# An attention softmax whose bias step delivers the negated maximum itself

## The chip, the cores and the metric

The kernel runs on one core of a Trainium2 chip. A core has a matrix engine (TensorE: PE in the profile, with its weight loads as PEld), a vector engine (VectorE, DVE), a scalar engine for activation functions (ScalarE, ACT), a general engine (GpSimd, POOL) and a sync engine (SP) that issues DMAs. Each engine works through a queue of its own in order; semaphores hold an instruction until what it reads is there or what it overwrites is free. The metric is the device time of one launch in microseconds (us), lower is better.

## The reference

One layer of a bidirectional encoder over 4096 tokens of width 1024. After a norm and one large input projection, two groups of heads work side by side: an mLSTM matrix memory in both directions, and windowed attention. Their outputs go through an output projection, a residual add and a last norm. The change touches the softmax of the windowed attention alone:

```
scores = einsum('bnqhgd,bnkhd->bnhgqk', qb, kw) * (B_HEAD_DIM ** -0.5)
scores = where(mask, scores + bias, NEG_INF)
m = maximum(max(scores, axis=-1), sink_l)
p = exp(scores - m[..., None])
denom = sum(p, axis=-1) + exp(sink_l - m)
out = einsum('bnhgqk,bnkhd->bnqhgd', p, vw) / denom
```

There are 32 blocks of 128 queries, 8 query heads that share 2 key heads, and each block sees its own and the two neighbouring blocks of keys. Each head has a learned logit, the sink, that takes part in the maximum and in the denominator.

## The kernel before

The kernel has three passes. Pass 1 (lines 168 to 678) normalises the input, projects q, k and v of the attention, and runs the attention. Pass 2 computes the memory's projections and its backward states, pass 3 the forward states, the gates and the output projection. The products use an fp32 value split into two parts (three matmuls for one product), which is why PE has so many.

The attention runs in 64 *slots*, one for each block of queries `n` and key head `kv` (`sl = 2n + kv`). `slot` (line 442) deals the pieces of three slots in turn, so that a slot's scores are computed two slots ahead of its transposes, and its products with the values one slot after them:

- `att_a(sl, g)`, four times in a slot: the scores of one group of 128 rows (two query heads by 64 queries). Two matmuls (line 379) fill one of two PSUM buffers `sp`; a DVE step (line 382) adds the table of position biases, writes the sums to an SBUF tile `s`, and gives each row's maximum through an accumulator that a second small instruction writes out. After the fourth group a DVE step (line 389) takes the minimum of the negated maxima and the negated sink, 128x4 values, into `NG`; then ACT (line 391) runs the exponential of the four groups one after another, with `NG` as its bias and the row sums as its accumulator.
- `att_t(sl, i)`, up to three times: four transposes on PE (line 411), then a rounded copy on ACT (413) and the remainder on DVE (414), both into a tile `pt`.
- `att_o(sl, i)`, up to three times: two matmuls with the values (line 425) into the one PSUM buffer `op`. After the last of them a copy on ACT (437) and an add on DVE (438) bring the result into `ab`, of which there is one buffer for both key heads; after the second key head SP issues its store to `at_d` in HBM (440).

These pieces are dealt between the projections of the next blocks of tokens (`interleave`, line 132): `qproj` (548), `kproj` (484), `vproj` (516, 517). Beside them the input of later blocks is prepared: ACT's squares (214), DVE (250) and POOL (251) give each row's scale; POOL stores it to HBM with one DMA for each 128 rows, a single value for each row (254, `rs_d`); SP loads it back spread over all partitions (261, `rsb`); POOL multiplies (266, `scale_raw`); ACT rounds (275) and POOL takes the remainder (276). Late in pass 1 DVE and ACT also prepare weights (683, 684) and gates (706 to 785); `sinks` (394) then adds the sink's share to the row sums, and DVE's reciprocal of them (785) opens pass 2.

The order of the work on PE is written out by hand. The order on all other engines, SP and POOL's DMAs included, comes from a planner that simulates the program when it is built: it takes what is ready by order in the program, with steps in a `high_priority` block put forward by `EV`, 400 places (lines 437 and 438 are in one). `behind(c, ins)` keeps instructions of the same engine behind a named one; `LAST["act"]` names the latest exponential, and the squares of line 214 and the weight casts of line 683 are kept behind it.

Of the kernel before, what the change touches and what calls it, by code (L numbers as in the profile page):

```python
# [9 lines left out]
F32 = mybir.dt.float32  # L10
F32R = mybir.dt.float32r
BF16 = mybir.dt.bfloat16
AF = mybir.ActivationFunctionType
ALU = mybir.AluOpType
# [14 lines left out]
def f32(ap):  # L29
    return ap.bitcast(F32)  # L30
# [54 lines left out]
def xtile(c, shape, dt, name):  # L85
    return c.xp.tile(shape, dt, tag="x4", name=name)
# [81 lines left out]
def pass1(c):  # L168
    nc, tc, A = c.nc, c.tc, c.A
    NB = 16  # L170
    with ExitStack() as es:
        wk = es.enter_context(tc.tile_pool(name="p1", bufs=1, reuse_waits="tile"))
        x_in, LAST = {}, {}
# [147 lines left out]
        def small_loads():  # L321
            r = {}
            r["gb"] = wk.tile([128, 2, 2, 4], F32, name="gb")
            nc.sync.dma_start(r["gb"], A["gate_b"].partition_broadcast(128).rearrange("p (a b d) -> p a b d", a=2, b=2))
            sink = r["sink"] = wk.tile([128, 2, 2, 2], F32, name="sink")
            for z in range(2):
                nc.sync.dma_start(sink[64 * z:64 * z + 64].rearrange("p a h m -> p (a h m)"),
                                  A["sink"][z].partition_broadcast(64))
            r["nsink"] = wk.tile([128, 2, 2, 2], F32, name="nsink")
            return [r[k] for k in ("gb", "sink", "nsink")]  # L330

        bias = []
# [25 lines left out]
        KK, Q, V, XT, ST = {}, {}, {}, {}, {}  # L358

        def att_a(sl, g):  # L360
            n, kv = sl // 2, sl % 2
            left, right = n > 0, n < NCH - 1
            jl, jr = (0 if left else 128), (384 if right else 256)
            b = (n + 1) // 2 if right else n // 2
            col = n * 128 - (b * 256 - 256)
            kk = KK[b]
            qb, qc = Q[n // 2], (n % 2) * 128
            half, m = g // 2, g % 2
            lo, hi = max(jl, 64 * half), min(jr, 320 + 64 * half)
            kept = lambda g: slice(max(jl, 64 * (g // 2)), min(jr, 320 + 64 * (g // 2)))  # L370
            if g == 0:
                st = wk.tile([128, 4], F32, tag="st", bufs=4, name=f"st{sl}")
                ST[sl] = ([], list(range(jl // 128, jr // 128)), st)
            ps, _, mx = ST[sl]
            ng, rs = c.NG[:, kv, n, :], c.R[:, n, kv, :]
            sp = c.ps("a", [128, 384], f"sp{sl}_{g}")
            qt = qb[kv * 2 + m][:, qc // 64 + half].rearrange("p z q -> p (z q)")
            for z in range(2):
                nc.tensor.matmul(sp[:, lo:hi], qt, kk[:, kv, z, col - 128 + lo:col - 128 + hi],  # L379
                                 start=(z == 0), stop=(z == 1))  # L380
            s = SB[half][(2 * sl + m) % 6]
            nc.vector.tensor_tensor_reduce(out=s[:, lo:hi], in0=sp[:, lo:hi],  # L382
                                           in1=bias[0][:, kv * 2 + m, lo - 64 * half:hi - 64 * half],
                                           op0=ALU.add, op1=ALU.max, scale=1.0, scalar=-3e38,
                                           accum_out=mx[:, g:g + 1])
            ps.append(s)
            if g < 3:
                return
            nc.vector.scalar_tensor_tensor(ng, mx, -1.0, nsink[:, kv].rearrange("p h m -> p (h m)"), ALU.mult, ALU.min)  # L389
            for g in range(4):  # L390
                LAST["act"] = nc.scalar.activation(ps[g][:, kept(g)], ps[g][:, kept(g)], AF.Exp, bias=ng[:, g:g + 1],  # L391
                                                   accum_out=rs[:, g:g + 1])

        def sinks():
            for kv in range(2):
# [6 lines left out]
        PT, AB, OP = {}, {}, {}  # L402

        def att_t(sl, i):
            ps, js, _ = ST[sl]
            if i >= len(js):
                return
            j = js[i]
            tp = c.ps("b", [128, 512], f"tp{sl}_{j}")
            for g in range(4):  # L410
                nc.tensor.transpose(tp[:, g * 128:(g + 1) * 128], ps[g][:, j * 128:(j + 1) * 128], c.ident)  # L411
            pt = PT[sl, i] = xtile(c, [128, 2, 512], F32R, f"pt{sl}_{j}")
            nc.scalar.copy(pt[:, 0, :], tp)  # L413
            nc.vector.tensor_sub(pt[:, 1, :], tp, f32(pt[:, 0, :]))  # L414
# [27 lines left out]
        def slot(sl):  # L442
            T = lambda i: (lambda: att_t(sl, i))
            O = lambda i: (lambda: att_o(sl - 1, i))
            Sc = lambda g: (lambda: att_a(sl + 2, g))
            p = [Sc(0), O(0), Sc(1), T(0), O(1), Sc(2), T(1), O(2), Sc(3), T(2)]
            if sl == 0:
                p = [Sc(0), Sc(1), T(0), Sc(2), T(1), Sc(3), T(2)]
            if sl + 2 >= 2 * NCH:
                p = [O(0), T(0), O(1), T(1), O(2), T(2)]  # L450
            return p
# [172 lines left out]
        gb, sink, nsink = small_loads()  # L624
# [15 lines left out]
        with behind(c, LAST["gather"]):  # L640
            load_rows(3)
        norm_rows(3, LAST["q"])
        interleave(kproj(1) + vproj(1) + transposes(2), [(lambda g=g, s=s: att_a(s, g)) for s in range(2) for g in range(4)])
        c.w2 = []
        with behind(c, LAST["gather"]):
# [1029 lines left out]
```

## Time and profile before

| | |
|---|---|
| median of 3 runs | 2187.8 us (2187.6 to 2189.53) |
| profiled execution, first to last instruction (span) | 2182.1 us |
| the median's time outside such a span | 5.7 us |
| instructions | 34919 |
| busy: PE, PEld | 2156.9 us (99%), 1872.4 us (86%) |
| busy: DVE, ACT, POOL | 1416.9 (65%), 1079.3 (49%), 567.7 us (26%) |
| mean granted TensorE clock | 0.998 |
| first and last sum step (line 382) | 35.6 and 572.0 us |

Of the profiled execution the span is what is known; what lies outside it is taken from the median of the runs. A row of the busy groups reads: line, engine, operation, tile written <- tiles read, shape, count | busy time and mean duration of one | idle time of the engine just before them, and what ended it. In a row of one line's instructions the three numbers behind the count are the shortest, median and longest duration in ns. A row of the timeline gives start, duration, engine, line and tiles, and in brackets the idle time before it with what released it.

### The profile page before, as it was taken

Reading aid. Unit: us, or ns where it says so; the run is one execution under the profiler, and the core shown is the slowest. Engines: PE = TensorE matmul, PEld = TensorE weight load, DVE = VectorE, ACT = ScalarE, POOL = GpSimd, SP = SyncE. Lnnn points to the kernel's source line nnn. Section 1 sums busy time; section 2 is a strip of 40 time slices with the busy share of each in tenths; the row PEclk is TensorE's granted clock in tenths of the full one; section 3 lists DMA queues with packets and bytes.
Section 4 is the critical chain, followed back from the end, with each engine's and each line's share of the span. In section 5 each row is a group of like instructions: output and inputs, shape, how many; then the busy total and the mean of one; then the engine's idle time right before and its main releaser. Section 6 shows DMA issues by size and latency. Waiting matters only on the chain. (4 is left out here: it accounts for less than half of the span.)

```text
span 2182.1 us, 34919 instructions
## 1 busy us (share of the span) xinstructions
PE 2156.9 (99%) x12226; PEld 1872.4 (86%) x12226; DVE 1416.9 (65%) x3041; ACT 1079.3 (49%) x2650; POOL 567.7 (26%) x918
## 2 busy tenths in 40 slices
PE   8999999999999999999999999999999999999998
PEld 7999999999898888888888888888888888888886
DVE  7678787788686566556567655555554443777786
ACT  7788788787554344334344544444443321333333
POOL 3555465550031121121112211121211111112222
PEclk9999999999999999999999999999999999999999
DMA  9655455332342454144357887677676998667775
GB/s 277 158 171 147 128 173 122 130 124 64 102 148 78 141 163 135 62 160 160 113 163 230 290 259 238 211 253 225 214 238 188 329 359 283 181 177 191 193 191 147
DMA packets 249132, 398.96 MB, mean 183 GB/s; under 512 B 21979, under 2 KB 128475, under 8 KB 248956
## 3 DMA queue, kind: packets, MB, share of 16 engines
q1 hardware_dynamic: 220544, 303.50, 45.4%
q0 software_dynamic: 28176, 92.96, 13.6%
q8 instruction: 96, 1.57, 0.3%
q14 instruction: 80, 0.66, 0.1%
q10 hardware_dynamic: 236, 0.27, 0.1%
HBM read 275.99 MB, written 120.67 MB: 182 GB/s over the span
## 5 line engine op out<-in xcount | busy, mean ns | idle before, releaser
L932 PE MATMUL up<-xb,w 128*128 128x512 f32 x1344 | 338.4, 396 | 0.0
L1443 PE MATMUL o<-wo,yo 128*128 128x512 f32 (+1 forms) x1356 | 312.8, 393 | 0.0
L1443 PEld LDWEIGHTS o<-wo,yo 128*128 128x128 f32 x1356 | 253.2, 188 | 59.7
L932 PEld LDWEIGHTS up<-xb,w 128*128 128x128 f32 x1344 | 243.8, 188 | 47.2
L950 DVE SCALAR_TENSOR_TENSOR qk<-U,cw,qk 128x512 f32<-128x512 f32 x256 | 189.2, 752 | 91.1 <-ACT qk L948 85.8
L548 PE MATMUL qp<-xT,wqb 128*128 128x256 f32 x1536 | 242.4, 288 | 0.1
L548 PEld LDWEIGHTS qp<-xT,wqb 128*128 128x128 f32 x1536 | 214.2, 190 | 8.7 <-DVE wqb L319 0.5
L1262 PE MATMUL op<-w,xs 128*128 128x512 f32 x720 | 202.3, 408 | 0.0
L1262 PE MATMUL zp<-w,xs 128*128 128x512 f32 x720 | 187.9, 401 | 0.7 <-DVE z L1272 0.7
L905 PE MATMUL v2p<-w,xb 128*128 128x512 f32 x672 | 157.6, 395 | 0.0
L1262 PEld LDWEIGHTS zp<-w,xs 128*128 128x128 f32 x720 | 130.9, 189 | 27.4 <-DVE z L1272 1.1
L414 DVE TENSOR_TENSOR pt<-tp,pt 128x512 fp32r<-128x512 f32 x188 | 129.1, 687 | 37.7 <-ACT pt L413 35.2
L905 PEld LDWEIGHTS v2p<-w,xb 128*128 128x128 f32 x672 | 126.1, 188 | 30.1 <-DMA xb<-xT_d 0.5
L391 ACT ACTIVATE s<-s,NG 128x320 f32<-128x320 f32 (+1 forms) x256 | 139.8, 548 | 11.4 <-DVE NG L389 10.8
L1262 PEld LDWEIGHTS op<-w,xs 128*128 128x128 f32 x720 | 126.7, 189 | 21.4
L413 ACT CAST pt<-tp 128x512 fp32r<-128x512 f32 x188 | 110.5, 588 | 69.9 <-PE tp L411 67.6
L382 DVE CUSTOM_DVE_ANT_0 s<-sp,G 128x320 f32<-128x320 f32 (+1 forms) x256 | 122.2, 478 | 32.6 <-PE sp L379 29.9
L1229 ACT ACTIVATE hs<-num,r 128x128 f32<-128x128 f32 x128 | 47.0, 368 | 174.3 <-DVE r L1226 153.6
L425 PE MATMUL op<-pt,v 128*128 128x512 f32 x376 | 120.6, 402 | 5.9 <-DVE ab L438 5.8
L379 PE MATMUL sp<-kk,q 128*128 128x320 f32 (+2 forms) x512 | 118.8, 313 | 0.7 <-DVE kk L501 0.6
L411 PE MATMUL tp<-ident,s 128*128 128x128 f32 x752 | 113.2, 273 | 0.3 <-DVE pt L414 0.2
L1252 POOL DMA_DIRECT2D y_d<-ya x32 | 19.4, 607 | 329.8 <-ACT ya L1251 181.8
(275 smaller groups left out, 4480.5 us busy)
## 6 DMA issues: line engine op xcount, KB each, us to landing
xc<-xT_d SPq DMA_DIRECT2D x64, 512.0 KB, 8.1
xs<-xT_d SPq DMA_DIRECT2D x120, 256.0 KB, 6.6
xT_d<-xT POOLq DMA_DIRECT2D x104, 256.0 KB, 5.0
xb<-xT_d SPq DMA_DIRECT2D x48, 514.0 KB, 8.0
E<-m_d SPq DMA_DIRECT2D x64, 256.0 KB, 4.9
W<-w_d SPq DMA_DIRECT2D x64, 256.0 KB, 5.9
y<-y_d SPq DMA_DIRECT2D x32, 512.0 KB, 3.4
out<-xr POOLq DMA_DIRECT2D x31, 512.0 KB, 3.7
```

What stands on the lines that cost most here:

```text
L379: nc.tensor.matmul(sp[:, lo:hi], qt, kk[:, kv, z, col - 128 + lo:col - 128 + hi], start=(z == 0), stop=(z == 1))
L382: nc.vector.tensor_tensor_reduce(out=s[:, lo:hi], in0=sp[:, lo:hi], in1=bias[0][:, kv * 2 + m, lo - 64 * half:hi - 64 * half], op0=ALU.add ...
L391: LAST["act"] = nc.scalar.activation(ps[g][:, kept(g)], ps[g][:, kept(g)], AF.Exp, bias=ng[:, g:g + 1], accum_out=rs[:, g:g + 1])
L411: nc.tensor.transpose(tp[:, g * 128:(g + 1) * 128], ps[g][:, j * 128:(j + 1) * 128], c.ident)
L414: nc.vector.tensor_sub(pt[:, 1, :], tp, f32(pt[:, 0, :]))
L425: nc.tensor.matmul(op, vt, pt[:, z, :], start=(i == 0 and z == 0), stop=(i == len(js) - 1 and z == 1))
L548: nc.tensor.matmul(qp, wq[k // 2][:, k % 2, w, m * 128:m * 128 + 128], x[k], start=(k == 0 and j == 0), stop=(k == KT - 1 and j == 2))
L905: nc.tensor.matmul(vp, a, wv[k // 2][:, k % 2, m, :], start=(k == 0 and j == 0), stop=(k == KT - 1 and j == 2))
L932: nc.tensor.matmul(up[:, 0:hi - lo], w[k // 2][:, k % 2, a, cs], x, start=(k == 0 and j == 0), stop=(k == KT - 1 and j == 2))
L950: nc.vector.scalar_tensor_tensor(acc, U[:, t:t + 512], cw[:, cm, t:t + 1], acc, ALU.mult, ALU.add)
L1262: nc.tensor.matmul(P[nm], XS[n](a, k), w[:, m, :], start=(k == 0 and j == 0), stop=(k == KT - 1 and j == 2))
L1443: nc.tensor.matmul(p, a[:, z, k, :], w[k // 2][:, k % 2, m, lo:hi], start=k == 0 and z == 1, stop=k == 3 and z == 0 and m == 0)
```

## The change

The sum step of line 382 now writes the negated sum (scale -1) and takes the minimum over it, starting from the negated sink of its rows, which it reads as one value for each partition; its accumulator is written to `NG` directly. The step of line 389 and the small tile `st` are gone. Each exponential follows its own sum step, with scale -1, instead of running after the fourth group.

```diff
             if g == 0:
-                st = wk.tile([128, 4], F32, tag="st", bufs=4, name=f"st{sl}")
-                ST[sl] = ([], list(range(jl // 128, jr // 128)), st)
-            ps, _, mx = ST[sl]
+                ST[sl] = ([], list(range(jl // 128, jr // 128)))
+            ps, _ = ST[sl]
...
             nc.vector.tensor_tensor_reduce(out=s[:, lo:hi], in0=sp[:, lo:hi],
                                            in1=bias[0][:, kv * 2 + m, lo - 64 * half:hi - 64 * half],
-                                           op0=ALU.add, op1=ALU.max, scale=1.0, scalar=-3e38,
-                                           accum_out=mx[:, g:g + 1])
+                                           op0=ALU.add, op1=ALU.min, scale=-1.0,
+                                           scalar=nsink[:, kv, half, m:m + 1], accum_out=ng[:, g:g + 1])
             ps.append(s)
-            if g < 3:
-                return
-            nc.vector.scalar_tensor_tensor(ng, mx, -1.0, nsink[:, kv].rearrange("p h m -> p (h m)"), ALU.mult, ALU.min)
-            for g in range(4):
-                LAST["act"] = nc.scalar.activation(ps[g][:, kept(g)], ps[g][:, kept(g)], AF.Exp, bias=ng[:, g:g + 1],
-                                                   accum_out=rs[:, g:g + 1])
+            LAST["act"] = nc.scalar.activation(s[:, kept(g)], s[:, kept(g)], AF.Exp, scale=-1.0, bias=ng[:, g:g + 1],
+                                               accum_out=rs[:, g:g + 1])
```

More of the change, by code (lines that the diff above doesn't have):

```diff
@@ L404, in att_t @@
         def att_t(sl, i):
-            ps, js, _ = ST[sl]
+            ps, js = ST[sl]
             if i >= len(js):
```

## The prediction

> **What bounds the kernel now.** I read the page first, then the busy time of each engine in long stretches, then who waited for whom on PE.
>
> ```profile
> span 2182.1 us, 34919 instructions
> ...
> PE 2156.9 (99%) x12226; PEld 1872.4 (86%) x12226; DVE 1416.9 (65%) x3041; ACT 1079.3 (49%) x2650; POOL 567.7 (26%) x918
> ```
> ```profile
> 35.00:120.00 85.00, 81.86 (x617) 78.57 (x616) 61.60 (x173) 66.59 (x180) 46.93 (x67) 0.98 0.75 189
> 120.00:480.00 360.00, 360.00 (x2744) 348.65 (x2742) 286.72 (x740) 288.58 (x761) 195.78 (x269) 1.00 0.45 135
> 480.00:600.00 120.00, 115.83 (x792) 105.54 (x791) 92.92 (x238) 81.65 (x210) 13.35 (x44) 1.00 0.29 94
> 600.00:2100.00 1500.00, 1497.88 (x7568) 1255.13 (x7567) 895.36 (x1750) 592.94 (x1403) 283.39 (x475) 1.00 0.64 199
> ...
> PE bps L336 <- POOL ohb L299: 6.4, 1, 6.4
> PE op L425 <- DVE ab L438: 5.8, 4, 2.5
> ```
>
> In the stretches the columns are busy PE, PEld, DVE, ACT and POOL, then the granted clock, the DMA share and GB/s. PE bounds the kernel: 99% of the span, and not one visible idle microsecond from 120 to 480, where most attention runs. DVE and ACT are at 80% there (286.72 and 288.58 of 360), so shortening them gains nothing by itself. What an edit to the attention steps can win is PE's idle time beside attention: 3.14 us in 35 to 120 and 4.17 us in 480 to 600. Of it 5.8 us are one wait: the matmul of line 425 needs its single PSUM buffer, which DVE's add of line 438 frees. The 6.4 us wait comes before attention. The span stands against a median of 2187.8 us; I add the 5.7 us outside the span to every result.
>
> **What the change removes.** 64 DVE instructions at line 389, and four exponentials stop waiting for the last of four sums.
>
> ```profile
> L382 DVE CUSTOM_DVE_ANT_0 s<-sp,G x256: 343/481/493, 35.6 to 572.0; 128x320 f32<-128x320 f32 x120, 128x192 f32<-128x192 f32 x4, 128x256 f32<-128x256 f32 x4
> ...
> L389 DVE SCALAR_TENSOR_TENSOR NG<-st,nsink x64: 144/162/1824, 39.6 to 572.9; 128x4 f32<-128x4 f32 x64
> ...
> L389 DVE SCALAR_TENSOR_TENSOR NG<-st,nsink 128x4 f32<-128x4 f32 x64 | 21.1, 330 | 1.5
> ...
> L391 ACT ACTIVATE s<-s,NG 128x320 f32<-128x320 f32 (+1 forms) x256 | 139.8, 548 | 11.4 <-DVE NG L389 10.8
> ```
>
> DVE loses 64 x 330 ns = 21.1 us, and ACT loses 10.8 us of waiting, both off PE's path: they lie beside a PE that is busy. The mean of 330 ns is twice the median of 162: some take 1.8 us, and one of those matters below. These 128x4 steps read two SBUF tensors, and the long ones lie under a POOL tensor step. [...]
>
> **What it adds.** The sum step of line 382 now reads its start value per partition. The trace has no such form; the nearest rows are steps with and without a per-partition scalar.
>
> ```profile
> L1022 DVE SCALAR_TENSOR_TENSOR C<-C,decay,kv x124: 331/343/351, 633.7 to 1167.4; 128x129 f32<-128x129 f32 x124
> ...
> L397 DVE TENSOR_TENSOR NG<-sink,NG 128x128 f32<-128x128 f32 x2 | 0.6, 289 | 1.2 <-ACT s L391 1.2
> ```
>
> 343 against 289 ns is about 55 ns. The other bound is 0: the old step also carries two constants. Below 0 I see no reason. I take 55, the row nearest in operands (PSUM, one SBUF tensor, one scalar): 256 x 0.055 = 14 us, so DVE's net is -7 us, or -21 us by the other bound. Row 1022 keeps within 20 ns over 124 steps, so a scalar from SBUF by itself makes no long steps. All this hides behind PE; where DVE is full for a slot, the four sums gain 0.22 us and the removed step gives back at least 0.15, so an uncovered slot costs under 0.1 us. The negated scale of sum and exponential, and the minimum for the maximum, change no count and no shape: 0. Exponentials and their accumulator reads stay 256 each.
>
> **What it moves.** The exponentials leave as four separate steps, not as a burst of some 2.2 us. They issue no DMA, but they stand in ACT's queue ahead of the copy of line 437, and after that copy come DVE's add (438) and the store on SP's queue (440). The steps queued behind the latest exponential by order of issue (the squares of line 214 and the weight casts of line 683) now name a nearer one; PE waits for neither in the table of waits: 0, and at most one exponential, 0.55 us, if that cover were gone. The largest visible PE wait is where this counts:
>
> ```profile
> 63.16 4.74 POOL L266 TENSOR_TENSOR xraw<-xraw,rsb 128x1024 f32<-128x1024 f32 x2 [15.68 <-DMA rsb<-rs_d]
> ...
> 63.82 1.74 DVE L389 SCALAR_TENSOR_TENSOR NG<-st,nsink 128x4 f32<-128x4 f32 x1
> ...
> 65.65 0.56 ACT L391 ACTIVATE s<-s,NG 128x320 f32<-128x320 f32 x1 [1.42 <-DVE NG L389]
> ...
> 65.94 0.62 PE L425 MATMUL op<-pt,v 128*128 128x512 f32 x2
> ...
> 68.87 1.14 POOL L254 DMA_DIRECT2D rs_d<-rstd  x2 [0.29 <-POOL rstd L251]
> 69.10 0.58 ACT L437 COPY ab<-op 64x512 f32<-64x512 f32 x1
> ...
> 69.72 0.69 DVE L438 TENSOR_TENSOR ab<-op,ab 64x512 f32<-64x512 f32 x1
> ...
> 70.44 0.33 SPq L440 DMA_DIRECT2D at_d<-ab  x1
> ...
> 79.91 0.58 ACT L437 COPY ab<-op 64x512 f32<-64x512 f32 x1 [2.70 <-DMA at_d<-ab]
> ...
> 80.53 0.68 DVE L438 TENSOR_TENSOR ab<-op,ab 64x512 f32<-64x512 f32 x1 [2.56 <-ACT ab L437]
> ...
> 81.27 0.98 PE L425 MATMUL op<-pt,v 128*128 128x512 f32 x2 [2.47 <-DVE ab L438]
> ...
> DMA to landing us min/median/max: 2.0/3.3/9.4
> ...
> 80.00:90.00 10.00, 8.73 (x53) 8.40 (x54) 5.75 (x17) 6.45 (x18) 6.65 (x9) 0.83 0.78 293
> ```
>
> Read it from the end. PE idles 2.47 us because the next copy into `ab` waits until the store of 70.44 has landed: 9.4 us after its issue, where the median store takes 3.3. POOL had issued two stores of single 4-byte values (`rs_d`) 1.6 us before it. The store was that late because the copy of 69.10 was late, though its matmuls ended at 65.94 + 0.62 = 66.56: ACT first stood 1.42 us for line 389, itself held for 1.74 us beside POOL, and then ran the burst. Without line 389, three of the four exponentials have gone before. ACT reaches the copy up to 1.42 + 3 x 0.55 = 3.07 us earlier, but not before 66.56; the store then leaves at 66.6 + 0.58 + 0.69 + 0.1 = 68.0, ahead of 68.87. Bounds: 68.0 and 70.44 (the planner may fill the place with other casts). With only the 1.42 us won it leaves at 69.0, just behind POOL's. I take the early side: the 1.42 us and one of the three exponentials suffice (1.97 against the 1.57 us between 68.87 and 70.44). At the median landing the buffer is free by 71.3, long before 77.2 (79.91 less 2.70), and the idle 2.47 us go.
>
> With them goes a clock drop: 0.83 over 10 us is 3.4 us at half speed, 1.7 us of work. [...]
>
> The second place is the end of the stage:
>
> ```profile
> 575.43 0.29 DVE L397 TENSOR_TENSOR NG<-sink,NG 128x128 f32<-128x128 f32 x1 [1.18 <-ACT s L391]
> ...
> 577.98 0.58 ACT L437 COPY ab<-op 64x512 f32<-64x512 f32 x1 [0.35 <-PE op L425]
> 578.31 1.74 DVE L785 RECIPROCAL R<-R 128x256 f32<-128x256 f32 x1
> 580.08 0.69 DVE L438 TENSOR_TENSOR ab<-op,ab 64x512 f32<-64x512 f32 x1
> ...
> 580.83 0.73 PE L425 MATMUL op<-pt,v 128*128 128x512 f32 x2 [2.19 <-DVE ab L438]
> ```
>
> DVE's add waits behind the 1.74 us reciprocal, whose chain starts at line 397 after the last burst. With the burst gone that chain starts at least 1.18 us sooner; if the reciprocal is then queued before the late work, the add starts at 578.56, 1.5 us earlier. If the order stays, 0. I take 1.0. The remaining waits (the 1 us near 550, where DVE is full of gate and weight work) I leave as they are: bounds -1.0 and +0.3.
>
> **Sum.** 2182.1 - 2.5 - 1.7 - 1.0 = 2176.9; plus 5.7 is 2182.6 us.
>
> **Rivals.** (B) The store stays behind POOL's: the planner puts casts of `xT` and `pt` where the burst was. For it: two such casts stand between burst and copy now, and all of ACT is dealt out by a planner I cannot see. Only the end gains: 2186.8 us.
>
> (C) Slower: an exponential queued ahead of the copy of line 437 holds it, since it now waits for its own sum, whose scores PE computes after the matmuls being copied.
>
> ```profile
> 247.81 0.67 PE L425 MATMUL op<-pt,v 128*128 128x512 f32 x2
> ...
> 248.51 0.51 PE L379 MATMUL sp<-kk,q 128*128 128x320 f32 x2
> ...
> 249.24 0.58 ACT L437 COPY ab<-op 64x512 f32<-64x512 f32 x1
> ...
> 249.48 0.48 DVE L382 CUSTOM_DVE_ANT_0 s<-sp,G 128x320 f32<-128x320 f32 x1
> ...
> 249.88 0.68 DVE L438 TENSOR_TENSOR ab<-op,ab 64x512 f32<-64x512 f32 x1
> ...
> 251.00 0.63 PE L425 MATMUL op<-pt,v 128*128 128x512 f32 x2
> ```
>
> The add ends at 250.56 and the next matmul starts at 251.00: 0.44 us of slack. An exponential behind the sum of 249.48 would run from 250.05 to 250.6, and the copy would be 1.36 us late: 0.9 us of PE idle in that slot. It decides once the copy is over 0.44 us late. In all 64 slots that is 59 us; in one of eight, 7.4 us: 2195.2. Against it: the copy and the add are issued with raised priority, and none of the slots from 120 to 480 stalls today, whatever lies beside them.
>
> (D) The busy PE hides waits: rows of matmuls overlap, so a wait under 0.2 us does not show. [...] If each of 64 slots hid 0.1 us that the spread exponentials free, 6.4 us more than the end's gain: 2180.4. Against it, two windows of steady work:
>
> ```profile
> 120.00:180.00 60.00, 60.00 (x459) 58.12 (x458) 47.47 (x122) 47.80 (x125) 31.29 (x40) 1.00 0.40 125
> ...
> 300.00:360.00 60.00, 60.00 (x458) 58.04 (x458) 49.74 (x127) 47.82 (x127) 35.66 (x49) 1.00 0.55 156
> ```
>
> The count of matmuls does not move while DVE and DMA do.
>
> **Chances.** The forecast 0.47, B 0.25, C 0.20, D 0.08. A measurement of this kernel cannot tell less than about 0.2% (4.4 us) from no change: below 2183.4 is faster. The forecast lies 0.8 us past that line; its own range is 2180.8 to 2184.7 (the end at 0 to 2.19, the first place between 2.5 and 4.2). I give it 0.33 faster, 0.13 the same, 0.01 slower; B 0.24 the same, 0.01 slower; C slower; D faster. Faster 0.41, same 0.37, slower 0.22. The range 2179.5 to 2191.0 takes in B, D and the mild half of C.
>
> **What would show it.** The clock over 80 to 90 us back at 1.00 and no PE idle there: the first place is right. `at_d` issued before `rs_d` but still landing in 9 us: the reading of POOL's stores is wrong. The reciprocal before 578.3: the second place. Sum steps of 540 ns: the scalar's price; spread up to 1.8 us: it contends with POOL. PE idle before line 425 between 120 and 480: C, and the forecast is wrong. New PE idle after 600, which no step here touches, would be the planner's reordering, and would make it wrong too.

## The result and the profile after

The changed kernel takes 2192.5 us (median of 10 runs, 2189.46 to 2197.11) against 2186.8 us of the kernel before on the same chip: 1.0028 times the time, with a 95% interval of 1.0017 to 1.0039. It is slower by 0.28%, where the forecast was 2182.6 us, with a gain as the likeliest of three outcomes (0.41). Its profiled execution took 2190.26 us, 1.7 us more than its span; its span is 6.5 us longer than before's. Its ten times form two groups of five, 2189.5 to 2190.6 us at a mean granted clock of 0.999 and 2194.4 to 2197.1 us at 0.997 or 0.998, and the profile is of the lower group.

The page after, and its busy time in the stretches that the prediction used (PE, PEld, DVE, ACT, POOL, granted clock, DMA share, GB/s):

```profile
span 2188.6 us, 34920 instructions
...
PE 2160.2 (99%) x12226; PEld 1872.1 (86%) x12226; DVE 1429.0 (65%) x2977; ACT 1089.2 (50%) x2650; POOL 566.3 (26%) x918
```
```profile
120.00:480.00 360.00, 358.70 (x2701) 344.43 (x2700) 290.32 (x686) 291.80 (x755) 191.52 (x265) 1.00 0.43 132
480.00:600.00 120.00, 114.66 (x776) 104.19 (x776) 93.63 (x229) 83.02 (x206) 15.23 (x45) 1.00 0.29 89
```

PE is still at 99%, and from 120 to 480 us it shows only 1.3 us of idle time, yet in those 360 us it runs 43 matmuls fewer than before (2701 against 2744). The time went where the idle column cannot show it. DVE has 64 instructions fewer and 12.1 us more to do. Two groups, in the view by line (busy time, mean) and then with their shortest, median and longest duration, say why:

```profile
L381 DVE CUSTOM_DVE_ANT_0 s<-sp,G,nsink 128x320 f32<-128x320 f32 (+1 forms) x256 | 138.1, 540 | 34.1 <-PE sp L378 29.3
...
L522 DVE TENSOR_TENSOR v<-vg,v 128x128 fp32r<-128x128 f32 x32 | 43.0, 1345 | 0.3 <-ACT v L521 0.2
```
```profile
L381 DVE CUSTOM_DVE_ANT_0 s<-sp,G,nsink x256: 407/550/555, 35.6 to 578.0; 128x320 f32<-128x320 f32 x120, 128x192 f32<-128x192 f32 x4, 128x256 f32<-128x256 f32 x4
...
L522 DVE TENSOR_TENSOR v<-vg,v x32: 281/1056/2469, 23.7 to 530.2; 128x128 fp32r<-128x128 f32 x32
```

The sum step went from 478 to 540 ns in the mean, close to its price. The other row is a step that the change never touched: the remainder of v (what is left of v after its rounded cast), which took 402 ns in the median before (28.4 us in all).

```profile
L527 DVE TENSOR_TENSOR v<-vg,v x32: 274/402/1911, 23.7 to 525.4; 128x128 fp32r<-128x128 f32 x32
```

PE issues the same 12226 matmuls in the same order in both kernels, so each can be compared by its start. The table gives, for matmuls of the products with the values and for the last matmul of all, how much later (+) or earlier (-) than in the kernel before they start, in us, in the profiled execution of each kernel named; the heads are the times of these matmuls in the kernel before. The fourth column is the slope between 132 and 435 us: by how much the lag grows in one block of four slots (33.6 us). The kernels e2 to e18 are those of the experiments below; in e4 PE has 66 matmuls between 49.6 and 76.6 us in another order, so there the products with the values are paired by their own order.

| kernel | at 54 | at 98 | slope per block | at 435 | at 587 | last |
|---|---|---|---|---|---|---|
| changed | +1.6 | -3.1 | +0.51 | +2.0 | +4.5 | +6.5 |
| e2 constant start | +2.0 | +0.9 | +0.46 | +5.5 | +7.8 | +8.2 |
| e4 rows later (softmax of before) | -0.2 | -3.3 | +0.02 | -3.1 | -1.2 | -1.3 |
| e5 held | +0.4 | -4.2 | +1.97 | +15.9 | +19.9 | +20.5 |
| e6 step kept | +0.5 | +1.3 | +0.48 | +5.6 | +7.8 | +8.3 |
| e7 v after add | +1.8 | +1.1 | +0.15 | +2.7 | +5.4 | +6.1 |
| e8 v on POOL | +1.5 | -3.2 | +0.16 | -1.6 | -0.1 | +1.0 |
| e9 fourth named | +1.7 | -3.0 | +0.51 | +2.1 | +2.1 | +2.9 |
| e14 all but rows | +0.5 | -3.2 | +0.16 | -1.7 | -2.3 | -1.8 |
| e15 step kept, constant | +0.1 | -0.9 | 0.00 | -0.9 | -0.9 | -1.0 |
| e17 e14 with constant | +0.3 | -2.9 | +0.04 | -1.6 | -1.7 | -0.9 |
| e18 e14 without held start | +1.8 | -3.1 | +0.15 | -1.6 | -2.3 | -1.0 |

The changed kernel thus loses 1.6 us before 54 us (at 45.3 us PE idles 1.59 us for `kk`, the split keys), wins 4.7 by 98 us, loses 5.1 in the ten blocks to 435 us, 2.5 more to the end of the attention, and 1.9 in the passes behind it. The gain is the first place of the prediction; here are its rows after, and the same ten microseconds as there:

```profile
67.55 0.62 PE L420 MATMUL op<-pt,v 128*128 128x512 f32 x2
...
69.52 0.58 ACT L432 COPY ab<-op 64x512 f32<-64x512 f32 x1
...
70.92 0.33 SPq L435 DMA_DIRECT2D at_d<-ab  x1
71.24 1.14 POOL L254 DMA_DIRECT2D rs_d<-rstd  x2
```
```profile
80.00:90.00 10.00, 10.00 (x77) 9.65 (x77) 7.86 (x19) 6.96 (x18) 6.57 (x14) 1.00 0.92 234
```

The store `at_d` now goes ahead of POOL's stores and lands 2.03 us after its issue instead of 9.4; the idle 2.47 us and the half clock (in the kernel before 0.50 from 82 to 85 us, and 1.00 again from 85) are gone. But it goes ahead by 0.32 us, not by the 0.9 that the prediction had, and later than before (70.92 against 70.44). The loss is seen best in one slot:

```profile
246.96 0.67 PE L420 MATMUL op<-pt,v 128*128 128x512 f32 x2
...
247.16 0.30 DVE L518 TENSOR_TENSOR vg<-vp,vg 128x144 f32<-128x144 f32 x1
247.26 0.56 ACT L386 ACTIVATE s<-s,NG 128x320 f32<-128x320 f32 x1
...
247.81 0.61 ACT L275 CAST xT<-xraw 128x512 fp32r<-128x512 f32 x1
...
248.32 0.30 ACT L521 CAST v<-vg 128x128 fp32r<-128x128 f32 x1
248.50 1.10 POOL L276 TENSOR_TENSOR xT<-xraw,xT 128x512 fp32r<-128x512 f32 x1
248.64 0.58 ACT L432 COPY ab<-op 64x512 f32<-64x512 f32 x1
...
248.69 1.05 DVE L522 TENSOR_TENSOR v<-vg,v 128x128 fp32r<-128x128 f32 x1
...
249.66 0.67 DVE L433 TENSOR_TENSOR ab<-op,ab 64x512 f32<-64x512 f32 x1
...
250.39 0.74 PE L420 MATMUL op<-pt,v 128*128 128x512 f32 x2
```

The same slot before, beside the rows that the prediction showed for it:

```profile
248.67 0.30 DVE L523 TENSOR_TENSOR vg<-vp,vg 128x144 f32<-128x144 f32 x1
...
249.66 1.08 POOL L276 TENSOR_TENSOR xT<-xraw,xT 128x512 fp32r<-128x512 f32 x1
249.72 0.30 ACT L526 CAST v<-vg 128x128 fp32r<-128x128 f32 x1
...
250.49 0.40 DVE L527 TENSOR_TENSOR v<-vg,v 128x128 fp32r<-128x128 f32 x1
```

Before, v's split (cast and remainder) stood behind the copy into `ab` and behind the add. After, it stands ahead of both. The remainder starts at 248.69 beside POOL's step of 248.50 and ends 0.14 us after that step (249.74 against 249.60); before it did the same (250.89 against 250.74), but started late in POOL's step, and the add was already ahead of it. Now the add of 249.66 is behind it, and the next matmul into `op` starts as soon as that add is done. The row of that matmul has no bracket: none of this wait shows as idle time of PE. The slot stands for all: from 120 to 480 us there are two remainders of v in each block, and one of the two comes directly behind an add in all ten blocks of the kernel before, and directly ahead of one in all ten of the changed kernel.

### The profile page after: what moved, and what is told of

It reads as the page before. It is cut to its first block, busy times and chain, and to the rows that moved or that the text cites. A ratio compares the mean times of both kernels' runs of the same rounds, so it can differ in the third digit from the quotient of the medians.

```text
span 2188.6 us, 34920 instructions
## 1 busy us (share of the span) xinstructions
PE 2160.2 (99%) x12226; PEld 1872.1 (86%) x12226; DVE 1429.0 (65%) x2977; ACT 1089.2 (50%) x2650; POOL 566.3 (26%) x918
## 5 line engine op out<-in xcount | busy, mean ns | idle before, releaser
L381 DVE CUSTOM_DVE_ANT_0 s<-sp,G,nsink 128x320 f32<-128x320 f32 (+1 forms) x256 | 138.1, 540 | 34.1 <-PE sp L378 29.3
L378 PE MATMUL sp<-kk,q 128*128 128x320 f32 (+2 forms) x512 | 118.5, 312 | 0.6 <-DVE kk L496 0.6
```

## The experiments

The first theory, Q: an exponential now stands ahead of the copy into `ab` (the prediction's rival C, at a small size). Theory P: the dearer sum makes DVE late. A third, M, came out of the first runs: with the burst gone, other work (v's split, casts) has come to stand ahead of the copy and the add.

### Exponentials put back in the text, and the sum without its pointer

e1 issues the four exponentials behind the fourth group in the program; e3 issues them in pairs; e2 leaves them as they are, and takes the pointer away, so that the sink is left out of the maximum (the pointer is the start value that the sum reads for each partition).

```diff
 e1
-            LAST["act"] = nc.scalar.activation(s[:, kept(g)], s[:, kept(g)], AF.Exp, ...)
+            for i in range(4) if g == 3 else ():
+                LAST["act"] = nc.scalar.activation(ps[i][:, kept(i)], ps[i][:, kept(i)], AF.Exp, ...)
 e3
+            for i in (g - 1, g) if g % 2 else ():
 e2
-                                           scalar=nsink[:, kv, half, m:m + 1], accum_out=ng[:, g:g + 1])
+                                           scalar=3e38, accum_out=ng[:, g:g + 1])
```

> The new sum step stays, but the four exponentials go again as one burst after the fourth sum. Theory Q (place in ACT's queue: an exponential wedged ahead of the copy into ab delays DVE's add and the next op matmul by some 0.1 to 0.25 us a slot): the steady loss of 0.5 us per block of four slots from 120 to 480 us is gone, the 1.6 us lost before 54 us is gone, and the time is 2184 to 2187, at or below the kernel before. Theory P (price: the sum step of 540 instead of 480 ns makes DVE late in each slot): the steady loss stays at about 0.5 us per block and the time is 2190 to 2193. Theory O (the planner merely orders things otherwise, with no link to either): anything from 2184 to 2194, with the difference in one or two places rather than steady.

> The changed kernel with a constant start value (3e38) for the minimum in place of the per-partition negated sink: the sink is left out of the row's maximum. The sum step should go back to about 481 ns and DVE lose some 15 us of busy time. Theory Q: the exponentials still stand ahead of the copies, the steady loss of 0.5 us per block stays, and the time is 2190 to 2193. Theory P: the steady loss goes and the time is 2183 to 2186. If both share it: in between, 2187 to 2189.

> The changed kernel with the exponentials issued two by two, after the second and the fourth sum. The third group's scores come right after the op matmuls, so in this version no exponential of the third group is issued ahead of the copy into ab. Theory Q: most of the steady loss goes (under 0.2 us per block), the gains at 80 us (4 us) and at 578 us (1.5 us) stay, and the time is 2182 to 2187. Theory P: loss of 0.5 us per block stays, 2190 to 2193.

Measured against the kernel before (2185.3): e1 2189.7 us, ratio 1.0019 (1.0010 to 1.0028); e2 2191.3, 1.0027 (1.0018 to 1.0037); e3 2190.5, 1.0024 (1.0014 to 1.0035). The slope stays at 0.45, 0.46 and 0.47 us per block. Taken at its word this is against Q and P both. But e1 and e3 did not do what they were to do, as the timeline of e1 shows:

```profile
242.66 0.55 DVE L381 CUSTOM_DVE_ANT_0 s<-sp,G,nsink 128x320 f32<-128x320 f32 x1
...
243.26 0.56 ACT L387 ACTIVATE s<-s,NG 128x320 f32<-128x320 f32 x1 [0.30 <-DVE NG L381]
```

Each exponential still starts right behind its own sum: the planner takes what is ready, and only the data (before, all four minima in one step) had made them a burst. So e1 and e3 leave the move untried. e2 did get its sum of 480 ns, and the slope is 0.46. But the rest did not stay as it was: the planner there also puts one exponential and one cast of `pt` ahead of the copy into `ab` in each block, where the changed kernel has them behind it. So the pointer's share of the 0.51 cannot be read from e2 alone.

### The move undone by force, the step kept, and v's split

```diff
 e5
+            if g < 3:
+                return
+            last = None
+            for i in (3, 0, 1, 2):
+                with behind(c, last):
+                    LAST["act"] = nc.scalar.activation(ps[i][:, kept(i)], ...)
+                last = last or LAST["act"]
 e6
-                                           scalar=nsink[:, kv, half, m:m + 1], accum_out=ng[:, g:g + 1])
+                                           scalar=nsink[:, kv, half, m:m + 1], accum_out=mx[:, g:g + 1])
+            nc.vector.scalar_tensor_tensor(ng, mx, 1.0, nsink[:, kv].rearrange("p h m -> p (h m)"), ALU.mult, ALU.min)
 e7 (called in att_o, right after the add)
+                def split():
+                    with behind(c, LAST.get("abc")), behind(c, LAST.get("abv")):
+                        nc.scalar.copy(vt[:, :, 0:64], vv)
+                        nc.vector.tensor_sub(vt[:, :, 64:128], vv, f32(vt[:, :, 0:64]))
 e8
-                nc.vector.tensor_sub(vt[:, :, 64:128], vv, f32(vt[:, :, 0:64]))
+                nc.gpsimd.tensor_tensor(out=vt[:, :, 64:128], in0=vv, in1=f32(vt[:, :, 0:64]), op=ALU.subtract)
```

> In e1 and e3 the traces show each exponential still starting right behind its own sum: the place in the program text does not hold it back, so neither of them undid the move. Here the exponential of the fourth group goes first and the other three are queued behind it, so all four leave as a burst after the fourth sum, while the separate step between sums and exponentials stays removed and the sum keeps its new form. Theory M (the move: with the burst gone, ACT does v's split and the casts ahead of the copy into ab, and DVE's residual of v, held beside POOL, ahead of the add): the steady loss of 0.5 us per block and the 1.6 us before 54 us go, the time is within 2 us of the kernel before (2184 to 2187). Theory P (the removed step or the dearer sum): the loss stays, 2190 or more.

> The new sum step (negated, minimum, started from the negated sink; about 540 ns) writes to the small tile as before, and the separate 128x4 step between sums and exponentials is kept, so the exponentials are a burst again by their data. Everything of the change but the removal and the move. Theory M: no steady loss; time within 1.5 us of the kernel before, and the 9.4 us landing at 80 us is there again. Theory P (price of the sum): the loss of 0.5 us per block is there, 2189 to 2192.

> The changed kernel, with only this edit: in the blocks of the main loop, v's split (ACT's cast of 0.3 us and DVE's residual of 0.95 to 1.05 us) is queued behind the next copy into ab and add, where the kernel before had it. Theory M with this very step as the cause: the add starts 0.3 to 1.0 us sooner in one slot of four, the steady loss falls from 0.5 to 0.1 to 0.2 us per block, the time is 2186 to 2188 (some 4 us below the changed kernel). If the cause is spread over all the casts: a quarter of that at most, 2190 to 2191.

> The changed kernel with DVE's residual of v (128x128, two SBUF inputs) moved to POOL, nothing else. It tests the price of the residual itself: in the changed kernel each of them ends 0.15 us behind the POOL step that runs beside it (median 1.05 us, was 0.40). Theory M: DVE's busy time falls by about 29 us, the add no longer stands behind it, the steady loss falls to 0.2 us or less per block, time 2186 to 2188; POOL's next steps are later by 0.3 to 1 us, which nothing waits for. If the held residual is not the cause: 2190 to 2192.

e7 measured 2187.5 us, ratio 1.0013 (1.0004 to 1.0022), and e8 2187.4, 1.0008 (0.9999 to 1.0017). In both the slope falls from 0.51 to 0.15 and 0.16 us per block, as theory M has it: one step, standing in front of the add, is 70% of the steady loss. e8 is the cleanest of all the runs: ACT's work is in the changed kernel's order in all 2650 places, v's cast still ahead of the copy, and DVE's is too but for the remainders that are gone. So it is the remainder on DVE that holds the slot, not the cast on ACT. The slot of above in e7, where the add no longer waits for it and the remainder itself takes 0.27 us:

```profile
251.84 0.68 DVE L433 TENSOR_TENSOR ab<-op,ab 64x512 f32<-64x512 f32 x1 [0.29 <-ACT ab L432]
...
252.44 0.27 DVE L527 TENSOR_TENSOR v<-vg,v 128x128 fp32r<-128x128 f32 x1
```

e7 also shows how narrow the gain at 80 us is. In its profiled execution `at_d` goes 0.56 us behind the first of POOL's stores and lands after 9.9 us, and the wait and the drop of the clock that the kernel before had there are back (ACT's copy waits 2.72 us for the store, and the clock is at 0.83 in the mean from 80 to 90 us, as before):

```profile
70.53 1.14 POOL L254 DMA_DIRECT2D rs_d<-rstd  x2
71.09 0.33 SPq L437 DMA_DIRECT2D at_d<-ab  x1
...
81.07 0.58 ACT L432 COPY ab<-op 64x512 f32<-64x512 f32 x1 [2.72 <-DMA at_d<-ab]
```
```profile
80.00:90.00 10.00, 7.58 (x44) 7.23 (x45) 4.87 (x14) 5.57 (x16) 5.59 (x12) 0.83 0.97 297
```

e5 fell out against every theory: 2203.8 us, 1.0086 (1.0072 to 1.0100). The slope is 1.97 us per block, and PE waits 15.3 us for `pt`:

```profile
PE tp L412 <- DVE pt L415: 15.3, 14, 1.2
```

The forced burst runs the last group first, which the kernel before did not, and DVE no longer has the order of before either; what of the 1.97 us is the burst and what the order was not separated. It does win 4.2 us by 98 us and lose only 0.4 before 54 us, which points to the exponentials as what costs the 1.6 us at the start; e11 and e14 below, which hold the exponentials of the first two slots alone, bear it out (0.0 and +0.5 us at 54 us).

By theory M e6 was to be as fast as the kernel before, and was not: 2193.0 us, 1.0032 (1.0020 to 1.0045). Its first three blocks from 132 us on take exactly as long as before (+1.3 us at 132 and at 235 us), then it loses 1.3 to 1.4 us each in three single blocks. Theory P, dismissed after e2, was back: with the step kept, DVE has to do both 540 ns sums and the step. e15, below, takes it up.

### The gain at 80 us alone

```diff
 e4 (kernel before)
+            rows = [lambda: norm_rows(b + 4, LAST["act"])]
-            A1 = slot(4 * b) + [lambda: norm_rows(b + 4, LAST["act"])]
+            A1 = slot(4 * b) + (rows if b else [])
-            A2 = slot(4 * b + 2) + slot(4 * b + 3)
+            A2 = slot(4 * b + 2) + ([] if b else rows) + slot(4 * b + 3)
```

> The kernel before, softmax untouched; only the first block's norm rows (whose rs_d stores of single 4-byte values stand ahead of the first at_d store) are issued one slot later than the first at_d. My reading of the place at 80 us: at_d lands in 2 to 4 us instead of 9.4, the 2.47 us of idle PE and the drop to half clock at 80 us go, and the time is 4 us below the kernel before (2182 to 2183). If the reading is wrong: at_d still lands in about 9 us, PE still idles at 78 to 81 us, and the time is the kernel before's within 1 us.

Measured 2181.7 us against 2185.3, ratio 0.9982 (0.9973 to 0.9991): about the forecast's own time, with the softmax untouched. `at_d` is issued ahead of `rs_d` by 11.6 us and lands after 2.08 us, and no idle time or half clock is left from 80 to 90 us:

```profile
68.88 0.33 SPq L440 DMA_DIRECT2D at_d<-ab  x1
...
80.51 1.11 POOL L254 DMA_DIRECT2D rs_d<-rstd  x2
```
```profile
80.00:90.00 10.00, 10.00 (x79) 9.69 (x78) 7.17 (x19) 7.10 (x21) 2.95 (x8) 1.00 0.39 131
```

So the reading of this place was right, and the gain needs nothing of the change. Of the 4.2 us 3.1 are left (-0.2 at 54 us, -3.3 at 98), since PE now idles 1.23 us at 77.9 us for a transpose. The edit also shifts PE's own order between 49.6 and 76.6 us, so e4 is not a change of the stores alone. This version beats both kernels.

### The stage's end, and pieces together

e9 keeps the name of the fourth group's exponential for the weight casts and squares that are queued behind it:

```diff
-            LAST["act"] = nc.scalar.activation(s[:, kept(g)], s[:, kept(g)], AF.Exp, ...)
+            e = nc.scalar.activation(s[:, kept(g)], s[:, kept(g)], AF.Exp, ...)
+            if g == 3:
+                LAST["act"] = e
```

> The changed kernel, where the steps queued behind the latest exponential (the norm's squares and the weight casts of the stage's end) name the exponential of the fourth group again, as before, not the nearest. If the 3.6 us lost between 468 and 542 us come from those weight casts standing ahead of the copies into ab, that loss falls to 1 us or less and the time by 2 to 3 us against the changed kernel, 2188.5 to 2190. If the casts there come ahead for other reasons, the loss and the time stay (2190 to 2193).

Measured 2187.6 us, 1.0014 (1.0005 to 1.0023). From 435 to 587 us it loses nothing, where the changed kernel loses 2.5. In the changed kernel a weight cast stands right ahead of the copy at the stage's end (first fence), and its longest wait for the add was 1.6 us (second); with e9 it is 0.7 (third):

```profile
543.51 0.71 ACT L678 ACTIVATE w<-w2s,nw 128x512 fp32r<-128x512 f32 x1
...
544.12 0.56 ACT L432 COPY ab<-op 64x512 f32<-64x512 f32 x1
```
```profile
PE op L420 <- DVE ab L433: 5.2, 6, 1.6
```
```profile
PE op L422 <- DVE ab L435: 2.8, 6, 0.7
```

e10 to e12 put earlier edits together:

```diff
 e10: the changed kernel with the edits of e4 and e8
 e11: e10, and the first two slots' exponentials held as in e5
+            if sl < 2 and g < 3:
+                return
+            for i in (3, 0, 1, 2) if sl < 2 else (g,):
 e12: the kernel before with the edits of e4 and e8
```

> The changed kernel with two edits of earlier runs together: the first norm rows after the first at_d (as in e4) and v's residual on POOL (as in e8). The place at 80 us is then no race any more: whether at_d or rs_d is issued first no longer differs by 0.1 to 0.3 us from run to run. Expected: no half clock at 80 us in any run, the runs' spread under 3 us, the median at e8's undisturbed profile, 2184 to 2185.5, level with the kernel before. If the race was not what spreads the runs, the median stays at e8's 2187.

> As e10, and for the first two slots alone the exponentials are held as a burst behind the fourth sum (as in e5), so that none stands ahead of the casts of kk at 40 to 47 us. Expected: the 1.6 us lost before 54 us fall to 0.4, as in e5, and the time is 1 to 1.5 us below e10: 2183 to 2184.5. If the loss there has another cause: the same as e10.

> The kernel before, softmax untouched, with the two edits of e10 (first norm rows later, v's residual on POOL). Of its residuals 11 are held for 1.9 us, but not ahead of an add. If only what stands ahead of the copy and the add counts: within 1 us of e4, 2181 to 2182.5. If DVE's load as such counts (20 us of it go): 2 us or more below e4, under 2180.

Measured: e10 2187.9 us, 1.0015 (1.0007 to 1.0024); e11 2188.9, 1.0018 (1.0009 to 1.0026); e12 2184.2, 0.9992 (0.9983 to 1.0001). All three missed. e11's first part is right (0.0 at 54 us against e10's +1.2). What spoils them is the edit of e4, which also delays the chain behind the first norm rows. In e10 POOL's step of line 266 waits for `rsb`, a cast of ACT waits for POOL, the copy stands behind the cast, and PE idles 2.29 us at 110 us:

```profile
103.48 4.74 POOL L266 TENSOR_TENSOR xraw<-xraw,rsb 128x1024 f32<-128x1024 f32 x2 [7.92 <-DMA rsb<-rs_d]
...
105.91 0.62 ACT L275 CAST xT<-xraw 128x512 fp32r<-128x512 f32 x1 [2.67 <-POOL xraw L266]
...
108.65 0.58 ACT L432 COPY ab<-op 64x512 f32<-64x512 f32 x1
```

In e12 the next pair of `rs_d` stores goes ahead of the next `at_d` instead, and PE idles 3.35 us at 117 us. e16 is the changed kernel with that edit alone; e13 and e14 put all the pieces together, with and without it:

```diff
 e16: the changed kernel with e4's edit
 e13: the changed kernel with the edits of e7, e9, e11 and e4
 e14: e13 without e4's edit;   e18: e14 without e11's
```

> The changed kernel, only with the first norm rows issued after the first at_d. If the changed kernel's runs fall in two groups by the race at 80 us: one group here, within 3 us, and a median at its lower group, 2189 to 2190.5. If not the race: the same two groups as the changed kernel, up to 2197.

> The changed kernel with all four pieces taken away: v's split behind the copy and the add (e7), the fourth group's exponential named by the later steps (e9), the first two slots' exponentials held as a burst (e11), the first norm rows issued after the first at_d (e4). If the pieces add up, from the changed kernel's 2190.3 (its profiled time): 3.6 + 1.5 + 1.1 less, and no run with the half clock at 80 us: 2183 to 2185, level with the kernel before, above e4's 2181.7. If there is a cause not named yet, 2187 or more.

> As e13 but with the first norm rows where they were, so that the race at 80 us is there. If the race is what spreads the runs: single runs in two groups some 4 to 5 us apart, the lower at e13's time, the median 0 to 4 us above e13's.

e16 measured 2193.0 us, 1.0041 (1.0027 to 1.0054): no gain, PE now idles 1.19 us at 117 us behind an `at_d` that is late; and its six times reach from 2192.5 to 2196.9 us, so the race at 80 us is not shown to be what spreads the changed kernel's. e13 (v's split behind the add, the fourth named, the start held, the rows later) measured 2187.5, 1.0009 (1.0000 to 1.0018), and in its timeline the stall stands thus:

```profile
103.22 1.14 POOL L254 DMA_DIRECT2D rs_d<-rstd  x2
...
108.52 0.32 SPq L445 DMA_DIRECT2D at_d<-ab  x1
...
117.18 0.58 ACT L440 COPY ab<-op 64x512 f32<-64x512 f32 x1 [2.61 <-DMA at_d<-ab]
...
118.53 0.98 PE L428 MATMUL op<-pt,v 128*128 128x512 f32 x2 [2.06 <-DVE ab L441]
```

e14 is e13 without the rows' edit, and is what adds the pieces up: 2182.7 us, its 11 times within 2182.0 to 2184.2, ratio 0.9991 (0.9982 to 1.0000). By the ratios that is 8 us below the changed kernel, and level with or just below the kernel before. It keeps the new sum and the spread exponentials. e18 drops the held start from it:

> e14 without the held burst of the first two slots: v's split behind the add and the fourth exponential named. If the casts of kk only cost their own 1.1 us: one group of runs, a median of 2183.5 to 2184.5. If they also decide the race at 80 us: two groups some 4 to 5 us apart as in e7 and e9, the lower at 2183.5 to 2184.5, the upper at 2188.

Measured 2182.7 us, 0.9989 (0.9980 to 0.9998): the same, in one group. So the 1.6 us before 54 us cost nothing in the end: at 98 us both stand at -3.1 to -3.2. Two edits turn the change from a loss of 0.28% to a gain of 0.11%: v's split behind the add, and the name that the weight casts go by. Together they win more than e7 and e9 did singly (0.15 and 0.14%), and more than was expected of them; why is not shown.

### The price of the pointer

e15 is e6, e17 is e14, both with this; in e15 the sink still comes in by the kept step, and the order of work on PE, DVE, ACT and POOL is that of the kernel before in every place; e17 leaves the sink out of the maximum.

```diff
-                                           scalar=nsink[:, kv, half, m:m + 1], accum_out=...)
+                                           scalar=3e38, accum_out=...)
```

> As e6 (negated sum, minimum, separate step kept), but the sum starts from a constant (3e38); the sink still comes in by the separate step, so the computation is whole. Its order of work on every engine is the kernel before's. If e6's loss is the pointer's price: the sum is 480 ns again and the time is the kernel before's within 1 us (2184 to 2186). If negation or minimum cost something: the time stays near e6's, 2190 or more.

> e14 with the constant start value (3e38), which leaves the sink out of the row's maximum. If the dearer sum still delays the add in one slot of four (e14 still loses 0.15 us per block): that slope goes to 0.05 or less and the time is 1 to 2 us below e14, 2181 to 2182. If not: e14's 2182.7 within 0.5 us.

e15 measured 2185.6 us, 1.0004 (0.9995 to 1.0012): negating and taking the minimum cost nothing. e6 lies 7 us above it by the medians (6 by the ratios), and differs by the pointer alone; but with the pointer the planner also orders ACT's work otherwise in 90 places (casts of q, exponentials) and DVE's in 120. What of the 7 us is the longer step and what the order was not separated. The waits of e6, and then the sum's group and the waits of e15:

```profile
PE op L425 <- DVE ab L438: 7.3, 7, 3.0
```
```profile
L382 DVE CUSTOM_DVE_ANT_0 s<-sp,G 128x320 f32<-128x320 f32 (+1 forms) x256 | 122.4, 479 | 31.0 <-PE sp L379 28.3
```
```profile
PE op L425 <- DVE ab L438: 5.7, 4, 2.4
```

e17 measured 2181.2 us, 0.9982 (0.9973 to 0.9990), 1.4 us below e14 by the medians (2.0 by the ratios), with a slope of 0.04 instead of 0.16; here too the planner's order differs. So taking the same 60 ns away is worth 0.05 us per block where v's split holds the add anyway (e2), 0.12 where it does not (e17), and 0.48 where the separate step is still there (e15). A block has 16 sums, so 60 ns each would be 0.96 us: in none of the three do they come out at their own sum.

## Why the prediction was wrong, point by point

- **The base.** The 5.7 us outside the span were not there: the changed kernel's profiled execution took 1.7 us more than its span, and the median of the kernel before was 2184.8 to 2186.8 us in the comparisons. The forecast stood on a base 1 to 3 us too high; as a ratio (2182.6 of 2187.8, 0.9976) it was still on the wrong side. The forecast's "own range" of 2180.8 to 2184.7 does not follow from its bounds either: 2187.8 less 4.2 and 2.19 is 2181.4, and less 2.5 alone 2185.3.
- **The sum's price** was right in ns (55 forecast, 62 in the mean) and wrong in what it does. "All this hides behind PE", an uncovered slot "under 0.1 us": the pointer and the order that the planner makes of it cost 6 to 7 us in e6 against e15, 1.4 to 2.0 in e14 against e17. A busy share of 80% was taken for room. At 80% DVE has room on average, but the slot shown has it working from 246.08 to 250.33 us, the end of the add, with one gap of 0.13 us.
- **"Net -7 us" on DVE** came out as +12.1. The step's 21.1 us went and the sum's 15.9 us came (138.1 - 122.2); the term missing was above all v's remainder with 14.6 us (43.0 - 28.4). The prediction saw that the long steps lie under POOL's and asked whether the *sum* would get them (it did not: 407/550/555). It did not ask which other two-input steps could slide under POOL's. The sum of 14.6 us is not what was lost, though: in e7 the second remainder of each block still takes 2.5 us, and the slope falls all the same.
- **The move.** The step that failed: the exponentials were costed for what they do themselves, 0 or "at most one exponential, 0.55 us". What counts is what moved into the room they left: one step of DVE, 0.36 us in each block, which the sum has at nothing. In the slot shown, the add that makes v (line 518) starts 0.47 us before the last product ends (247.16 against 246.96 + 0.67 = 247.63); before, it came 0.19 us after that (248.67 against 247.81 + 0.67 = 248.48, as the prediction showed). So v's split is ready before the copy is, and the planner puts it first. That this order stands, and costs 70% of the slope, is shown (e7, e8); that the earlier v is its reason is read from these rows only.
- **LAST["act"]** "0, and at most one exponential, 0.55 us": 2.5 us by 587 us (e9). The prediction asked only whether PE waits for the weight casts themselves, not for whom they stand in front of.
- **The first place** was read rightly (e4: 3.6 us by the medians, against 4.2), and the changed kernel wins it in the profiled execution. But the term that carried it, a copy up to 3.07 us earlier, failed: the copy came at 69.52 instead of 69.10, because its products ended 1.6 us later (67.55 + 0.62 against 66.56). Behind them it came 1.2 us sooner than before (1.35 us after their end, where it had been 2.54), and the store won by 0.32 us. So the wait that was to go did go, but luck has a part in the place being won: e1, e2, e3 and e7 lose the same race by 0.56 to 1.50 us.
- **The second place** was won by the other order. The gain of 1.0 came out as 1.5 (the lag falls from 6.0 to 4.5 us from 571 to 587 us), but the reciprocal did not go first, it went behind the add:

```profile
578.38 0.68 DVE L433 TENSOR_TENSOR ab<-op,ab 64x512 f32<-64x512 f32 x1
...
580.95 1.74 DVE L780 RECIPROCAL R<-R 128x256 f32<-128x256 f32 x1
```

- **The rivals.** C had the right side and the right place, the copy into `ab` and the add behind it; its price (0.9 us in one slot of eight) and its actor (the exponential) were wrong: 0.36 us in one slot of four, by v's split, and more at the stage's end. Its condition, "once the copy is over 0.44 us late", asked for too much: the copy of 248.64 starts 1.01 us behind its product where it started 0.76 us behind (249.24 less 248.48), 0.25 us more, and DVE's own queue does the rest. And its sign, idle time of PE before the product with the values between 120 and 480 us, shows a single wait of 0.5 us where 5.1 were lost. D was right that the busy PE hides short waits (from 120 to 480 us each matmul in the profile of the kernel before overlaps the next by 0.16 to 0.25 us, and the changed kernel shows 1.3 us of idle time there beside its 5.1 us of lag), and had the sign wrong: they are new waits, not freed ones.
- **What stays open**: the 1.9 us that the changed kernel loses after 587 us (e9 loses 0.9, e14 about 0.5 there), of which one wait of 1.1 us in pass 3 is seen; what in e5 made 1.97 us per block; and why the changed kernel's ten times spread over 7.7 us, since one execution alone is profiled. A second buffer for `ab` or for `op` was not tried.

## What to carry to other kernels

When an edit takes a wait away, the first question is which ready work will fill the room, and what urgent step it will then stand in front of; a step that is cheap by its median (402 ns) can be the worst one to let pass if it lengthens beside another engine's step (here to as much as 2469 ns). Where a planner orders the queues, compare the position of the copy that frees the scarce buffer before and after, and pin it. And a gain that rests on which of two DMAs goes first should be won by order in the program (e4), not by a few tenths of a microsecond. Such an order has to be tried anew in each kernel: e4's edit won 3.6 us in the kernel before, and in e10, e12, e13 and e16 a new wait of 1.2 to 3.4 us came up between 110 and 119 us.

## What the runs showed of the hardware

- The remainder of v, a DVE step with two SBUF inputs, did not end before POOL's step of line 266 or 276 where that step ran when it started: it ended 0.145 to 0.158 us after that step, in all 23 such cases of the kernel before and all 24 of the changed one, up to 2.47 us long for 0.28 us of work. The sum, with one input from PSUM, one from SBUF and its start value from SBUF, showed nothing of the kind (407/550/555): of the 256 in the changed kernel 49 started during such a step, and they took 532 to 553 ns.
- A start value read per partition made this step 62 ns longer in the mean (478 to 540) and 69 in the median (481 to 550), most of them at 128x320.
- Whether the 256 KB store `at_d` is quick hung on POOL's stores of single 4-byte values: the first `at_d` landed 2.0 to 4.2 us after its issue in the 13 kernels that issue it ahead of the first `rs_d` of that place or at most 0.10 us behind it (e8), and 9.3 to 10.0 us in the seven that issue it 0.56 to 1.59 us behind (the kernel before, e1, e2, e3, e6, e7, e15). What holds it there is not shown.
- How long PE idled did not decide by itself whether its clock dropped: 2.47 us in the kernel before were followed by 0.50 from 82 to 85 us, and 2.06 us at 118.5 us in e13 by a lower clock too (0.89 in the mean of the ten us behind it), but the 2.35 us before 81.9 us in e15 were not (1.00). What does decide it is not shown. The row behind e13's wait, and then the one around e15's:

```profile
120.00:130.00 10.00, 10.00 (x71) 9.79 (x71) 7.64 (x16) 5.88 (x14) 6.07 (x7) 0.89 0.44 174
```
```profile
80.00:90.00 10.00, 8.11 (x62) 7.85 (x63) 6.74 (x18) 6.44 (x19) 5.91 (x8) 1.00 0.86 311
```
